# Attention and recurrence steps served in the same turn, value products joined with the next scores, statistics pinned behind the newest matmul, one head pair in another ring of banks

## The chip, the cores and the metric

The kernel runs on one core of one Trainium2 chip. The core has TensorE (PE, matmuls into the eight banks of PSUM), VectorE (DVE), ScalarE (ACT), GpSimd (POOL) and SyncE (SP), each with its own instruction queue, which it works through in order; semaphores tie them together. The metric is the device time of one execution in microseconds: 1956.87 us, the median of 3 runs.

## The reference

One step of a decoder layer for 1024 prompt tokens and 64 sample tokens (8 sequences of 8), model width 1024, all in float32:

```python
x = x + 0.5 * rms_norm(swiglu(rms_norm(x, norm_ffn1_pre), ffn1_w_gu, ffn1_w_down), norm_ffn1_post)
h = rms_norm(x, norm_mix_pre)
z = h @ w_in + b_in                      # q, k, v | hq, hf, hi, hg
a = rms_norm(window_attention(q, k, v, sinks), attn_out_norm)     # 8 heads of 64, 2 key heads, window 128
o = rms_norm(hgrn2_chunked(silu(hq), 1 - f, log f, hi, S0), hg_out_norm) * silu(hg)   # 4 heads of 128 x 128
x = x + rms_norm(concat(a, o) @ w_out, norm_mix_post)
x = x + 0.5 * rms_norm(swiglu(rms_norm(x, norm_ffn2_pre), ffn2_w_gu, ffn2_w_down), norm_ffn2_post)
```

Each feed-forward block has 2816 hidden columns with gate and up weights. The outputs are both token groups, the last 128 keys and values, and the recurrence's states. The sample tokens attend to a cache of 128 positions and start from given states; the prompt attends to its own block of 128 and the one before.

## The kernel before

The tokens form three parts: part 0 with 320 columns (256 prompt tokens and the 64 sample tokens), parts 1 and 2 with 384 prompt tokens each. A product of float32 numbers is made of three matmuls in a reduced format (`mm3`, L242 to L244): both operands are split in a high part (a cast on ScalarE, L219) and a low part (a subtraction on VectorE, L220), and high x high, low x high and high x low are added up in one bank. There are 10242 such matmuls, and they are the stream that everything else is put into. Weights come by DMA into three raw buffers, are split, and lie in a ring of eight tiles (four high and low pairs); a split waits until TensorE has used the pair four places before.

PSUM's eight banks form two rings of four: `mmbank` for the stream, `axbank` for the rest (scores, transposes, values, recurrence, statistics).

The program runs through these stages: the head of the first feed-forward block, twelve hidden tiles for part 0 alone (`up0`), while parts 1 and 2 are normalised (`pre_x`, called from the stream named p1); the rest of its up-projection (`up`); its down-projections (`down`, `pair`); then the middle part, in which projections (`w_in_units`, `w_out_units`), the last down-projections and the head of the second feed-forward block (`f2.head`, again `up0`) run while attention and recurrence are worked off; then the second feed-forward block.

Side work is written as generators, of which each `yield` ends a step. After every 12 matmuls or so (`proj` over four of eight inner tiles) the stream calls `tick`. It advances the named streams by their rates, and by `pace` two queues: "at" (attention blocks, 9 steps each) and "hg" (the recurrence). `pace` adds to each queue's `owed` the rate at which it must go to be done at its due tick (`DUE`), and takes a step of that queue whenever its own `owed` is 1 or more; the two queues are independent.

An attention block (`attn_block`) does its eight heads in two rounds of four. A round computes scores (L1163, two banks), reduces and exponentiates them, transposes the probabilities (L1189, two banks), and multiplies them with the values (L1204, into one bank that both rounds share). Behind the first round's value products stands a `yield`.

`bcast_steps` makes a norm's factor for a part whose tokens lie along the free axis: squares on ScalarE, sums on VectorE, a product with a column of 1/1024 (`st`, L294), then VectorE (L297), a power on GpSimd (L213), a diagonal on VectorE (`dg`, L304), two `yield`s, and a product with ones that spreads the factor over all partitions (`rb`, L308).

The program text does not fix the order on an engine: a scheduler with a model of the machine orders the instructions of each queue as their inputs become ready in that model, and an order that is written as `tc.issue_after(x)` is kept.

Of the kernel before, what the change touches and what calls it, by code (L numbers as in the profile page):

```python
# [18 lines left out]
P = 128  # L19
# [8 lines left out]
NPB = [2, 3, 3]  # L28
# [16 lines left out]
def tile_step(ctx: ExitStack, tc: tile.TileContext, A: dict, O: dict):  # L45
# [63 lines left out]
    def pace():  # L109
        now[0] += 1  # L110
        for k, q in queues.items():
            sofar, rate = 0, 0.0
            for n, _, left in q:
                sofar += left
                rate = max(rate, sofar / max(1, DUE[n] - now[0]))
            owed[k] += rate
            while owed[k] >= 1.0:
                owed[k] -= 1.0
                if q:
                    step(q)  # L120

    def need_mix(n):
        while any(q and q[0][0] <= n for q in queues.values()):
# [116 lines left out]
    def mm3(out, a, b, first, last, resume=False):  # L240

        PE.matmul(out, a[0], b[0], start=first, stop=False, skip_group_check=resume)  # L242
        PE.matmul(out, a[0], b[1], start=False, stop=False, skip_group_check=resume)  # L243
        return PE.matmul(out, a[1], b[0], start=False, stop=last, skip_group_check=resume)  # L244

    def hcol(h, k, w):
        return h[0][k // 4][:, k % 4, :w], h[1][k // 4][:, k % 4, :w]
# [25 lines left out]
    def bcast_steps(part, w, out, q=None, add=None):  # L273

        ss = tmp2("ss")
        for d in range(KC):
            if d == 0:
                S.activation(ss[:, :w], part(d), AF.Square)
                continue
            sq = tmp2("sq")  # L280
            S.activation(sq[:, :w], part(d), AF.Square)  # L281
            (add or V).tensor_tensor(ss[:, :w], ss[:, :w], sq[:, :w], op=ALU.add)
            if d % 3 == 0:
                yield
        yield
        nb = (w + P - 1) // P
        bank = axbank("st")
        sm = small()
        full = w // P
        if w % P:  # L290
            V.memset(sm[:, 0, 0:nb], 1.0)
        for c in range(nb):
            n = min(P, w - c * P)
            PE.matmul(bank[:n, c:c + 1], ss[:, c * P:c * P + n], omean, start=True, stop=True)  # L294
        for r, c in [(P, slice(0, full))] + ([(w % P, slice(full, nb))] if w % P else []):
            if q is None:
                V.tensor_scalar(sm[:r, 0, c], bank[:r, c], EPS, None, op0=ALU.add)  # L297
            else:
                V.scalar_tensor_tensor(sm[:r, 0, c], q[:r, c], EPS, bank[:r, c], op0=ALU.mult, op1=ALU.add)
        root(sm[:, 1, 0:nb], sm[:, 0, 0:nb])  # L300
        dg = tmp2("dg")
        for c in range(nb):
            n = min(P, w - c * P)
            V.tensor_scalar(dg[:, c * P:c * P + n], ident[:, :n], sm[:, 1, c:c + 1], None, op0=ALU.mult)  # L304
        yield
        yield
        rb = axbank("rb")
        PE.matmul(rb[:, :w], ones, dg[:, :w], start=True, stop=True)  # L308
        out.append(rb)
        yield  # L310

# [335 lines left out]
    def make_ffn(wgu, wdn, h, tag):  # L647
# [25 lines left out]
                f.stored = nc.sync.dma_start(acts[:, j], t[:, :w])  # L673
            return rest

        def up0(j, wts, after=None, mid=None):
            w = WIDTH[0]
            g, u = mmbank(), mmbank()
            for bank in (g, u):
                wt = wts.next()  # L680
                parts = (range(4), range(4, 8)) if mid is None or bank is g else (range(4), range(4, 7), range(7, 8))
                for ks in parts:
                    with tc.issue_after(after) if after is not None else nullcontext():
                        r = proj(bank[:, :w], wt, h[0], w, ks)
                    after = after and r.ins
                    if len(ks) == 3:
                        after = mid(after)
                    tick()
                if bank is g and mid is None:
                    rest = gated0(j, g)  # L690
            if mid is not None:
                rest = gated0(j, g)
            rest(u)
# [319 lines left out]
    def mixing(tp, h):  # L1013
# [132 lines left out]
        def attn_block(n, b):  # L1146
# [12 lines left out]
            for pr in range(2):  # L1159
# [37 lines left out]
                for i in range(2):  # L1197
                    for g in range(2):
                        c = (2 * pr + i) * P + 64 * g
                        for kb in range(nk):  # L1200
                            vb = b + kb + (1 if first else 0)
                            for q0 in (0, 64):
                                k1 = (i * nk + kb) * P + q0
                                PE.matmul(ob[q0:q0 + 64, c:c + 64], pT[g][:, k1:k1 + 64],  # L1204
                                          vn[:, vb, g * 64:g * 64 + 64], start=kb == 0, stop=kb == nk - 1)
                if pr == 0:
                    yield
            V.tensor_tensor(sm[:, 2], sinkb, sm[:, 0], op=ALU.subtract)
            S.activation(sm[:, 2], sm[:, 2], AF.Exp)
            V.tensor_tensor(mx[:, 2], mx[:, 1], sm[:, 2], op=ALU.add)  # L1210
# [276 lines left out]
        def ready(kind, n):  # L1487
            if n not in MT:
                MT[n] = new_h(n)
            if kind == "at":  # L1490
                gens = [(attn_block(n, b), 9) for b in range(NPB[n])]
                if n == 0:
                    gens += [(sample_attn(), 11), (kv_out(0), 1)]
                if n == 2:
                    gens.append((kv_out(2), 1))
            else:
                gens = [(intra(n), 8)] + [(hgrn_block(n, b), 3) for b in range(NPB[n])]
                if n == 0:
                    gens.append((sample_hgrn(), 14))
                if n == 2:  # L1500
                    gens.append((state_out(), 1))
# [92 lines left out]
    with tc.tile_pool(name="f1", bufs=1) as tp:  # L1594
# [10 lines left out]
        for i, j in enumerate(first[2:]):  # L1605
            if i == 1:
                with tc.issue_after(f1.stored.ins):
                    xs[2] = load_x(2)
            f1.up0(j, w0)
        f1.begin(units(HEAD1))  # L1610
        need("p1")
        f1.up({6: later(mix_consts), 8: misc, NJ - 1: f1.begin_down})
# [172 lines left out]
```

## Time and profile before

| | |
|---|---|
| runs | 1954.75, 1956.87, 1956.9 us |
| profiled execution | 1956.5 us, span 1954.6 us |
| TensorE busy | 1943.6 us (99%), mean granted clock 0.999 |
| VectorE, ScalarE, GpSimd busy | 1362.4, 929.5, 215.2 us |
| DMA | 358.20 MB, mean 183 GB/s |

The span runs from the first to the last instruction, the execution's time holds some us around it. A row of the timeline has start, duration, engine, line, operation and tiles; in brackets stands idle time of the engine before it and what ended it. In a row of the groups stand busy time and mean duration (ns), then idle time before the group. A matmul's duration overlaps the next one's; the spacing of starts tells the pace.

### The profile page before, as it was taken

The numbers are of one execution on the slowest core, as the hardware profiler recorded it, in microseconds if no ns is written. First come the engines' busy times: TensorE is split into PE (matmuls) and PEld (weight loads), VectorE is DVE, ScalarE is ACT, GpSimd is POOL, SyncE is SP. The second block draws the span as 40 slices with busy tenths as digits, with TensorE's granted clock in tenths as the row PEclk, the third lists the DMA queues.
The fourth block names the chain that finished last, engine by engine and source line by source line (L and its number), as shares of the span: only waits on it lengthen the run. The fifth ranks groups of instructions, "written<-read, shape, count | busy, mean of one in ns | idle before, by whom it ended". The sixth has DMA issues, their size and how long they took to land.

```text
span 1954.6 us, 34186 instructions
## 1 busy us (share of the span) xinstructions
PE 1943.6 (99%) x13469; PEld 1829.0 (94%) x13469; DVE 1362.4 (70%) x2206; ACT 929.5 (48%) x1627; POOL 215.2 (11%) x213
## 2 busy tenths in 40 slices
PE   9999999999999999999999999999999999999998
PEld 9999999999998987788899998999999999999887
DVE  7976667776558666876577576755987877655666
ACT  5533333444455545654345555655544444444453
POOL 0000000000004012121232124011000000000202
PEclk9999999999999999999999999999999999999999
DMA  7443344556767546665434343556555645667874
GB/s 257 147 153 147 134 168 173 183 188 213 245 215 231 183 135 185 214 222 143 132 111 148 97 126 123 165 159 208 171 200 193 217 174 184 210 237 228 309 261 142
DMA packets 160396, 358.20 MB, mean 183 GB/s; under 512 B 16284, under 2 KB 59996, under 8 KB 160220
## 3 DMA queue, kind: packets, MB, share of 16 engines
q1 hardware_dynamic: 159228, 354.19, 54.5%
q8 instruction: 105, 1.72, 0.4%
q10 hardware_dynamic: 1008, 1.84, 0.3%
q14 instruction: 55, 0.45, 0.1%
HBM read 279.33 MB, written 77.63 MB: 183 GB/s over the span
## 4 chain that ended last, share of the span: by engine, by line
PE 97%; DVE 1%; ACT 1%; DMA 0%; issue 0%; SPq 0%; DVEq 0%; POOLq 0%; POOL 0%; ACTq 0%
PE mm L242 29%; PE mm L244 29%; PE mm L243 29%; PE c L242 1%; PE c L244 1%; PE c L243 1%; PE sc L1163 1%; PE pv L1204 1%; PE lv L1237 1%; PE pT L1189 1%; PE av L1338 0%; PE u L1344 0%; PE l L1277 0%; PE av L1341 0%; DMA big<-in_x0T_dram 0%
## 5 line engine op out<-in xcount | busy, mean ns | idle before, releaser
L242 PE MATMUL mm<-h,wsph 128*128 128x320 f32 (+1 forms) x1296 | 416.3, 322 | 2.6 <-ACT sq L281 2.6
L243 PE MATMUL mm<-h,wsph 128*128 128x320 f32 (+1 forms) x1296 | 410.1, 317 | 0.0
L244 PE MATMUL mm<-h,wspl 128*128 128x320 f32 (+1 forms) x1296 | 408.6, 316 | 0.0
L220 DVE TENSOR_TENSOR wspl<-raw,wsph 128x1024 fp32r<-128x1024 f32 x200 | 251.0, 1256 | 151.0 <-ACT wsph L219 146.1
L219 ACT CAST wsph<-raw 128x1024 fp32r<-128x1024 f32 x200 | 209.1, 1047 | 279.2 <-PE mm L243 223.1
L219 ACT CAST w<-raw 128x512 fp32r<-128x512 f32 (+1 forms) x226 | 169.6, 754 | 255.6 <-PE mm L243 127.9
L220 DVE TENSOR_TENSOR w<-raw,w 128x512 fp32r<-128x512 f32 (+1 forms) x226 | 196.5, 873 | 85.2 <-ACT w L219 84.7
L242 PEld LDWEIGHTS mm<-h,wsph 128*128 128x128 f32 x1296 | 244.0, 188 | 10.9 <-issue 6.2
L243 PEld LDWEIGHTS mm<-h,wsph 128*128 128x128 f32 x1296 | 244.1, 188 | 0.8
L244 PEld LDWEIGHTS mm<-h,wspl 128*128 128x128 f32 x1296 | 243.7, 188 | 0.3
L242 PE MATMUL mm<-h,w 128*128 128x384 f32 x704 | 235.6, 335 | 0.0
L243 PE MATMUL mm<-h,w 128*128 128x384 f32 x704 | 235.6, 335 | 0.0
L244 PE MATMUL mm<-h,w 128*128 128x384 f32 x704 | 230.6, 335 | 0.0
L242 PE MATMUL mm<-w,h 128*128 128x512 f32 x462 | 181.2, 395 | 0.0
L243 PE MATMUL mm<-w,h 128*128 128x512 f32 x462 | 180.3, 391 | 0.0
L244 PE MATMUL mm<-w,h 128*128 128x512 f32 x462 | 178.3, 390 | 0.2 <-DVE h L220 0.2
L213 POOL TENSOR_TENSOR sm<-sm,mhalf 128x3 f32<-128x3 f32 (+4 forms) x37 | 37.5, 1013 | 1201.7 <-DVE sm L297 517.7
L242 PEld LDWEIGHTS mm<-h,w 128*128 128x128 f32 x704 | 132.2, 188 | 0.2 <-ACT big L763 0.2
L243 PEld LDWEIGHTS mm<-h,w 128*128 128x128 f32 x704 | 132.1, 188 | 0.0
L244 PEld LDWEIGHTS mm<-h,w 128*128 128x128 f32 x704 | 131.8, 188 | 0.0
L219 ACT CAST w<-t 128x512 fp32r<-128x512 f32 x176 | 106.9, 621 | 49.5 <-PE mm L244 45.8
L220 DVE TENSOR_TENSOR w<-t,w 128x512 fp32r<-128x512 f32 x176 | 118.9, 687 | 11.6 <-ACT w L219 11.6
(339 smaller groups left out, 3686.6 us busy)
## 6 DMA issues: line engine op xcount, KB each, us to landing
raw<-in_ffn_w_gu_dram SPq DMA_DIRECT2D x154, 512.0 KB
raw<-in_ffn_w_down_dram SPq DMA_DIRECT2D x74, 512.0 KB
raw<-in_w_in_dram SPq DMA_DIRECT2D x54, 512.0 KB
ar<-fa SPq DMA_DIRECT2D x70, 384.0 KB
big<-in_ffn_w_down_dram SPq DMA_DIRECT2D x88, 256.0 KB
fb<-big SPq DMA_DIRECT2D x44, 512.0 KB
raw<-fb SPq DMA_DIRECT2D x40, 512.0 KB
fa<-big SPq DMA_DIRECT2D x22, 768.0 KB
```

The costliest lines, as they stand in the source:

```text
L213: G.tensor_tensor(y, x, mhalf[:y.shape[0], :y.shape[1]], op=ALU.pow)
L219: S.copy(hi, src)
L220: return (lo_eng or V).tensor_tensor(lo, src, hi.bitcast(F32), op=ALU.subtract)
L242: PE.matmul(out, a[0], b[0], start=first, stop=False, skip_group_check=resume)
L243: PE.matmul(out, a[0], b[1], start=False, stop=False, skip_group_check=resume)
L244: return PE.matmul(out, a[1], b[0], start=False, stop=last, skip_group_check=resume)
L1163: PE.matmul(banks[g][:, i * 256:i * 256 + wk], zq[64 * g:64 * g + 64, 2 * pr + i, b * P:(b + 1) * P], kx[64 * g:64 * g + 64, k0:k0 + wk], ...
L1189: PE.transpose(bank[:, (i * nk + kb) * P:(i * nk + kb + 1) * P], pt[g][:, i, kb * P:(kb + 1) * P], ident)
L1204: PE.matmul(ob[q0:q0 + 64, c:c + 64], pT[g][:, k1:k1 + 64], vn[:, vb, g * 64:g * 64 + 64], start=kb == 0, stop=kb == nk - 1)
L1237: PE.matmul(b4[ps_, j, a], x[:, a, cs], y[:, a, cs], start=True, stop=True)
```

## The change

Five edits:

1. `pace` no longer serves each queue for itself. When both `owed` together reach 2, or one reaches 1.5, each queue takes one step in the same turn; an empty queue's account is set to 0.
2. In `attn_block` the `yield` behind the first round's value products is gone, so these and the second round's scores belong to one step; the block counts 8 steps.
3. In `bcast_steps` the products `st` and `rb` are pinned behind the matmul of the stream that was written last (`latest`), and a third `yield` stands before `rb`.
4. `up0` takes a function for its banks; the third hidden tile of the first head takes its two banks from `axbank`.
5. `mm3` notes its last matmul in `latest`.

```diff
@@ pace
-            while owed[k] >= 1.0:
+        while sum(owed.values()) >= 2.0 or max(owed.values()) >= 1.5:
+            for k, q in queues.items():
                 owed[k] -= 1.0
                 if q:
                     step(q)
+                else:
+                    owed[k] = 0.0
@@ mm3
-        return PE.matmul(out, a[1], b[0], start=False, stop=last, skip_group_check=resume)
+        r = latest[0] = PE.matmul(out, a[1], b[0], start=False, stop=last, skip_group_check=resume)
+        return r
+
+    latest = [None]
@@ bcast_steps
-            PE.matmul(bank[:n, c:c + 1], ss[:, c * P:c * P + n], omean, start=True, stop=True)
+            with tc.issue_after(latest[0].ins):
+                PE.matmul(bank[:n, c:c + 1], ss[:, c * P:c * P + n], omean, start=True, stop=True)
...
         yield
         yield
+        yield
         rb = axbank("rb")
-        PE.matmul(rb[:, :w], ones, dg[:, :w], start=True, stop=True)
+        with tc.issue_after(latest[0].ins):
+            PE.matmul(rb[:, :w], ones, dg[:, :w], start=True, stop=True)
@@ up0
-        def up0(j, wts, after=None, mid=None):
+        def up0(j, wts, after=None, mid=None, bank_of=mmbank):
             w = WIDTH[0]
-            g, u = mmbank(), mmbank()
+            g, u = bank_of(), bank_of()
@@ attn_block
-                if pr == 0:
-                    yield
@@ ready
-                gens = [(attn_block(n, b), 9) for b in range(NPB[n])]
+                gens = [(attn_block(n, b), 8) for b in range(NPB[n])]
@@ the first head
-            f1.up0(j, w0)
+            f1.up0(j, w0, bank_of=mmbank if i else axbank)
```

Lines behind the edits move by up to 9. How the order on the engines changes is shown at three places; what stands in brackets are the semaphores that an instruction waits for, by the engine that raises them.

The first place is TensorE in the first head, where the third hidden tile begins (`mm_352` and `ax_352` are its gate bank, `rb` the factor of part 0). Before:

```order
L631 MATMUL rb_330<-dg_258,ones 128x320 [waits DVE_49]
L242 MATMUL mm_272<-h_122,wsph_246 128x320
L243 MATMUL mm_272<-h_124,wsph_246 128x320
L244 MATMUL mm_272<-h_122,wspl_247 128x320
L242 MATMUL mm_352<-h_121,wsph_264 128x320 [waits DVE_49,Activation_49]
L243 MATMUL mm_352<-h_123,wsph_264 128x320
L244 MATMUL mm_352<-h_121,wspl_265 128x320
```

Now:

```order
L640 MATMUL rb_330<-dg_258,ones 128x320 [waits DVE_49]
L245 MATMUL mm_272<-h_122,wsph_246 128x320
L246 MATMUL mm_272<-h_124,wsph_246 128x320
L247 MATMUL mm_272<-h_122,wspl_247 128x320
L245 MATMUL ax_352<-h_121,wsph_264 128x320 [waits Activation_49]
L246 MATMUL ax_352<-h_123,wsph_264 128x320
L245 MATMUL ax_353<-h_121,wsph_275 128x320 [waits Activation_49]
L246 MATMUL ax_353<-h_123,wsph_275 128x320
L247 MATMUL ax_352<-h_121,wspl_265 128x320 [waits DVE_49]
```

The first matmul into the bank waits for the cast alone, no longer for VectorE too; the first that waits for VectorE is the one that reads the low part, and two matmuls of the up bank stand ahead of it.

The second place is TensorE and VectorE later in the same head, at the statistics of part 2 (`st_721`, `rb_765` before, `st_733`, `rb_777` now). On TensorE before, 26 matmuls lie between `st` and `rb`; here are the rows around `st`:

```order
L243 MATMUL mm_785<-h_124,wsph_659 128x320
L244 MATMUL mm_785<-h_122,wspl_660 128x320
L242 MATMUL mm_785<-h_122,wsph_659 128x320
L294 MATMUL st_721<-omean,ss_643 128x1 [waits DVE_49,PE_49]
L294 MATMUL st_721<-omean,ss_643 128x1 x2
L243 MATMUL mm_785<-h_124,wsph_659 128x320
```

Now:

```order
L246 MATMUL mm_782<-h_124,wsph_702 128x320
L247 MATMUL mm_782<-h_122,wspl_703 128x320
L301 MATMUL st_733<-omean,ss_664 128x1 [waits DVE_49]
L301 MATMUL st_733<-omean,ss_664 128x1 x2
L317 MATMUL rb_777<-dg_740,ones 128x384 [waits DVE_49]
L245 MATMUL mm_856<-h_121,wsph_749 128x320 [waits DVE_49,Activation_49]
```

On VectorE before:

```order
L297 TENSOR_SCALAR sm_722<-st_721 128x3 [waits PE_49]
L291 MEMSET sm_5681 128x3
L291 MEMSET sm_5863 128x3
L304 TENSOR_SCALAR dg_728<-ident,sm_722 128x128 [waits Pool_49]
L304 TENSOR_SCALAR dg_728<-ident,sm_722 128x128 x2
L668 TENSOR_TENSOR sg_744<-mm_701,rbs 128x320
```

Now (the cast of `wsph_860` waits for the matmul L246 of the rows above, `sg_744` frees the bank that `mm_856` takes):

```order
L304 TENSOR_SCALAR sm_734<-st_733 128x3 [waits PE_49]
L297 MEMSET sm_5681 128x3
L297 MEMSET sm_5897 128x3
L223 TENSOR_TENSOR wspl_861<-raw_858,wsph_860 128x1024 [waits DMAHW2_49,Activation_49]
L311 TENSOR_SCALAR dg_740<-ident,sm_734 128x128 [waits Pool_49]
L311 TENSOR_SCALAR dg_740<-ident,sm_734 128x128 x2
L677 TENSOR_TENSOR sg_744<-mm_698,rbs 128x320 [waits DMAHW0_49]
```

The two products of the statistics stand next to each other, and the split of a weight tile stands between VectorE's first step after `st` and the diagonal.

The third place is the head of the second feed-forward block, near the end of the middle part. On ScalarE before (`sg_13325` is the Silu that reads gate bank `mm_13253`, `h_13353` the cast of half of part 2's normalised tile):

```order
L469 ACTIVATE big_13163<-tr_13246,cols 128x384 [waits PE_49]
L666 ACT_TABLE_LOAD
L666 ACTIVATE sg_13325<-mm_13253 128x320
L1134 ACTIVATE junk,sm_13315<-t_1866_13313 128x512 [waits DVE_49]
L1128 CAST h_10478<-big_11126 128x4x128 [waits DVE_49]
L219 CAST wsph_13409<-raw_13407 128x1024 [waits DMAHW0_49,PE_49,Activation_49]
L666 ACTIVATE sg_13405<-mm_13373 128x320 [waits PE_49]
L483 CAST h_13353<-big_13163 128x1536 [waits DVE_49,Activation_49]
```

Now (`sg_13326` reads gate bank `mm_13262`, which `mm_13439` takes next):

```order
L1201 COPY t_1859_13253<-pT_13248 128x512 [waits PE_49,Activation_49]
L478 ACTIVATE big_13198<-tr_13255,cols 128x384 [waits PE_49]
L222 CAST wsph_13443<-raw_13441 128x1024 [waits DMAHW1_49,PE_49,Activation_49]
L492 CAST h_13353<-big_13198 128x1536 [waits DVE_49,Activation_49]
L675 ACT_TABLE_LOAD
L675 ACTIVATE sg_13326<-mm_13262 128x320
L675 ACTIVATE sg_13405<-mm_13373 128x320
```

And on TensorE now (the cast above waits for VectorE's copy of `tr_13321`):

```order
L247 MATMUL mm_13374<-h_11046,wspl_13267 128x320
L1213 MATMUL pv_13150<-vn_10030,t_1857_13246 64x64 [waits DVE_49]
L1213 MATMUL pv_13150<-vn_10030,t_1857_13246 64x64 x3
L473 MATMUL tr_13321<-ident,big_12313 128x128 [waits PE_49]
L473 MATMUL tr_13321<-ident,big_12313 128x128 x2
L1213 MATMUL pv_13150<-vn_10030,t_1859_13253 64x64 [waits Activation_49]
L1213 MATMUL pv_13150<-vn_10030,t_1859_13253 64x64 x3
L1213 MATMUL pv_13150<-vn_10030,t_1857_13246 64x64 x4
L1213 MATMUL pv_13150<-vn_10030,t_1859_13253 64x64 x4
L245 MATMUL mm_13439<-h_11045,wsph_13330 128x320 [waits Activation_49]
```

The Silu that frees the bank stood ahead of the large cast and stands behind it now, and between the transposes and the matmul that takes the bank stand twelve value products.

Over the whole program the small operations of TensorE form 160 islands between matmuls of the stream before and 141 now.

## The prediction

> **What bounds the kernel now.** I read the head of the page first, then the groups by line, then the waits.
>
> ```profile
> span 1954.6 us, 34186 instructions
> PE 1943.6 (99%) x13469; PEld 1829.0 (94%) x13469; DVE 1362.4 (70%) x2206; ACT 929.5 (48%) x1627; POOL 215.2 (11%) x213
> PE 97%; DVE 1%; ACT 1%; DMA 0%; issue 0%; SPq 0%; DVEq 0%; POOLq 0%; POOL 0%; ACTq 0%
> L242 PE MATMUL mm<-h,wsph 128*128 128x320 f32 (+1 forms) x1296 | 416.3, 322 | 2.6 <-ACT sq L281 2.6
> ```
>
> TensorE is busy 1943.6 of 1954.6 us and is 97% of the chain that ended last. Its main group of matmuls shows one wait in the whole program, 2.6 us. So the time can change in two ways only: TensorE does the same matmuls with less lost at their seams, or it stands still at other places than before. The profiled execution took 1956.5 us, 1.9 more than its span and 0.4 under the median of the runs (1956.87); I make the sum against 1956.5. A measurement of this kernel tells 0.2% (3.9 us) from no change.
>
> The 2.6 us have a place:
>
> ```profile
> 23.85 0.31 PE L243 MATMUL mm<-h,wsph 128*128 128x320 f32 x1
> 24.00 0.31 PE L244 MATMUL mm<-h,wspl 128*128 128x320 f32 x1
> 26.87 0.39 PE L242 MATMUL mm<-h,wsph 128*128 128x320 f32 x1 [2.56 <-ACT sq L281]
> ...
> 24.49 0.49 DVE L632 COPY rbs<-rb 128x320 f32<-128x320 f32 x1
> ...
> 25.16 1.17 DVE L220 TENSOR_TENSOR wspl<-raw,wsph 128x1024 fp32r<-128x1024 f32 x1
> 26.24 0.88 DVE L668 TENSOR_TENSOR sg<-mm,rbs 128x320 f32<-128x320 f32 x2
> ```
>
> The profile names a square of ScalarE as releaser, but matmul 26.87 starts 0.2 us after the first of the two L668 at 26.24 can have ended (0.44 us each). L668 reads the bank that the matmul wants to write; the squares on ScalarE have nothing to do with it. What this stop costs beyond itself is in the stretches around it (span in us, TensorE busy with its count, granted clock, DMA share, GB/s):
>
> ```profile
> 23.78:27.20 3.42, 0.86 (x6) 1.00 0.78 205
> 27.20:30.61 3.41, 3.41 (x15) 0.50 0.71 258
> 30.61:34.02 3.41, 3.41 (x25) 1.00 0.78 239
> ```
>
> In the stretch after the one in which TensorE was busy 0.86 of 3.42 us, its granted clock is 0.50: 15 matmuls where the next stretch holds 25, that is 3.41 / 2 = 1.7 us lost.
>
> **The change part by part.** *A. Head in idle banks.* The pair of banks wanted at 26.87 now comes from the other ring, where two of four banks are unused then. Without the bank, the matmul needs its weights alone:
>
> ```profile
> 17.16 1.98 ACT L219 CAST wsph<-raw 128x1024 fp32r<-128x1024 f32 x2
> 20.23 1.05 ACT L219 CAST wsph<-raw 128x1024 fp32r<-128x1024 f32 x1 [1.09 <-PE st L619]
> ...
> 22.22 2.36 DVE L220 TENSOR_TENSOR wspl<-raw,wsph 128x1024 fp32r<-128x1024 f32 x2
> ```
>
> High parts of both tiles are there at 19.1 and 21.3, low parts at 23.4 and 24.6; the first low part is asked for at about 24.6. So the stop goes: 26.87 - 24.00 - 0.15 (the spacing of these matmuls, 24.00 less 23.85) = 2.7 us, and the slow stretch with it, 1.7: **-4.4**. The other end is -2.7, for a stretch of low clock that not every execution has. What is late next: 48 matmuls later, at about 31.2, TensorE wants the bank that L668 frees at 26.7, so that stays covered.
>
> *B. Statistics pinned behind the newest matmul, one more turn before the broadcast.* Before, between the sum of squares (st) of the third part and its broadcast (rb) lay 26 matmuls of the head. In the new order st and rb stand together, and in VectorE's row the split of a weight tile stands between the first step after st and the diagonal (dg) that rb needs.
>
> ```profile
> 68.06 0.31 PE L242 MATMUL mm<-h,wsph 128*128 128x320 f32 x1
> 68.21 0.72 PE L294 MATMUL st<-omean,ss 128*128 128x1 f32 x6
> 68.79 0.39 PE L243 MATMUL mm<-h,wsph 128*128 128x320 f32 x1
> ...
> 68.97 0.16 DVE L297 TENSOR_SCALAR sm<-st 128x3 f32<-128x3 f32 x1 [1.58 <-PE st L294]
> ...
> 69.21 0.85 POOL L213 TENSOR_TENSOR sm<-sm,mhalf 128x3 f32<-128x3 f32 x1 [29.47 <-DVE sm L297]
> ...
> 70.09 0.68 DVE L304 TENSOR_SCALAR dg<-ident,sm 128x128 f32<-128x128 f32 x3 [0.94 <-POOL sm L213]
> ```
>
> From the start of the last matmul before st (68.06) TensorE goes on after 0.73 us. The diagonal is done after 70.77 - 68.06 = 2.71 at best: a stop of 2.0. With the split between, whose tile is freed by that very matmul: 0.2 until its end, cast 1.05 and split 1.18 (the rows under A), diagonal 0.68, some 0.05 at each hand-over, together 3.25: a stop of 2.5. I take **+2.5** (2.0 to 2.5), as the order puts the split there. Behind rb waits all of TensorE's queue, and VectorE's scaling by rb after it. The second part's broadcast keeps 31 matmuls between, some 4.6 us.
>
> *C. Swapped rows on ScalarE near the end of the middle part.* In the new order the cast of a 128x1536 tile stands before the Silu that reads a head bank; before, it stood six rows behind it. That cast waits for VectorE's copy of three transposes, which TensorE runs just before it wants the bank.
>
> ```profile
> L467 DVE TENSOR_SCALAR big<-tr,cols 128x384 f32<-128x384 f32 x8 | 4.9, 614 | 2.6 <-PE tr L464 2.6
> ...
> L483 ACT CAST h<-big 128x1536 fp32r<-128x1536 f32 x8 | 11.7, 1476 | 2.7 <-DVE big L436 2.1 <-DVE big L495 0.7
> ...
> L666 ACT ACT_TABLE_LOAD x7 | 9.0, 1283 | 0.1
> L666 ACT ACTIVATE sg<-mm 128x320 f32<-128x320 f32 x22 | 9.5, 432 | 0.1
> ```
>
> After the transposes: 0.16 until their result stands, 0.61 + 1.48 + 1.28 + 0.43, with four hand-overs 4.1 us. TensorE has 12 value products left for that time, some 0.9 to 1.0 us (a run of 16 costs 1.28 with both its seams, below). **+3.1** (2.5 to 3.3). That no such stop is in the trace of before agrees with its order, where the Silu was not behind the cast.
>
> *D. Other places.* The pairing moves the small operations of attention and recurrence on VectorE and ScalarE by up to a tick. No transfer is added or removed, SyncE's row has as many issues as before, and ScalarE loads its table 28 times in place of 32. Where these engines have no slack, TensorE stops briefly, as it does now already:
>
> ```profile
> 817.84 0.40 PE L243 MATMUL mm<-w,h 128*128 128x512 f32 x1
> 818.45 0.66 PE L1189 MATMUL pT<-ident,t 128*128 128x128 f32 x4 [0.22 <-DVE h L424]
> 819.32 0.50 PE L244 MATMUL mm<-w,h 128*128 128x512 f32 x1 [0.21 <-DVE h L220]
> ...
> 80.00:100.00 20.00, 20.00 (x138) 20.00 (x137) 20.00 (x19) 13.18 (x14) 0.00 (x0) 1.00 0.47 144
> ```
>
> 1.48 us from the first to the third row, in which four transposes stand that take 0.66 with their run-out: some 0.7 lost. And from 80 to 100 us VectorE is busy 20.00 of 20: a head that comes there 2 us earlier (4.4 less 2.5) may have to give some of it back. Bounds -0.8 (before's own loss goes) and +3; I take **+1.0**, nearest to what one such place costs.
>
> *E. Fewer seams.* Small operations stand as islands in the stream of matmuls. Their price, alone and merged:
>
> ```profile
> 1044.86 0.33 PE L243 MATMUL mm<-h,wsph 128*128 128x384 f32 x1
> 1045.03 0.34 PE L244 MATMUL mm<-h,wspl 128*128 128x384 f32 x1
> 1045.30 1.15 PE L1204 MATMUL pv<-vn,t 128*64 128x64 f32 x32
> ...
> 1046.66 0.34 PE L243 MATMUL mm<-h,wsph 128*128 128x384 f32 x1
> ...
> 1150.54 0.31 PE L244 MATMUL mm<-h,wspl 128*128 128x320 f32 x1
> ...
> 1151.99 0.31 PE L243 MATMUL mm<-h,wsph 128*128 128x320 f32 x1
> ...
> 1157.85 0.31 PE L244 MATMUL mm<-h,wspl 128*128 128x320 f32 x1
> ...
> 1160.38 0.31 PE L243 MATMUL mm<-h,wsph 128*128 128x320 f32 x1
> ```
>
> Value products alone: 1.63 less two spacings of 0.173 = 1.28. Levels alone (1150.54 to 1151.99): 1.45 - 0.29 = 1.16. Both in one island (1157.85 to 1160.38): 2.53 - 0.29 = 2.24. A merge saves 0.20 us. It pays only where two kinds of small products meet that use part of the array (scores, value products, levels). Such meetings are 6 in the order of before and 20 in the new one: 14 x 0.20 = 2.8. Against it, value products are cut by transposes at a few more places; I take **-2.5** (0 to -3.8, the latter if all 19 islands fewer paid).
>
> *F. Low clock after B and C.* The row of 23.78 to 27.20 says that 0.86 us of work in one stretch of 3.4 is too little. A stop of 3.1 leaves no more than that in one stretch in (3.41 - 3.1 + 2 x 0.55) / 3.41 = 41% of the positions that the stretches can have, one of 2.5 at most in 27%. 0.68 x 1.7 = **+1.2** (0 to 3.4).
>
> The Trainium skill, TensorE: Matmul & The Clock Gate (Part 1, the clock gate), has the clock halved after at least one idle window of about 3.4 us. By it neither B nor C would cost any clock and the sum would be 1.2 lower; this trace halved it after a stop of 2.7 us, so the row decides.
>
> Sum: 1956.5 - 4.4 + 2.5 + 3.1 + 1.0 - 2.5 + 1.2 = **1957.4 us**, 0.5 over the median of before.
>
> **The rivals.** *Faster.* B and C do not stand on the chip, or only one: 1956.5 - 4.4 - 2.5 + 1.0 = 1950.6 without both, 1953 to 1954 with one. For it: in the trace of before TensorE nearly never waits, so the order is made with knowledge of such waits. Against it: the chains are made of rows, and TensorE executes its row in order. Chance 0.20.
>
> *Slower, by banks.* A step now issues value products and the next scores at once, and the recurrence's step with them, on a ring of four banks: two for scores, one held for values, one left. The next taker waits for VectorE:
>
> ```profile
> L1171 DVE CUSTOM_DVE_ANT_0 t<-sc,amask 128x256 f32<-128x256 f32 x56 | 20.6, 421 | 5.6 <-PE sc L1163 5.5
> ```
>
> Four of these free a pair of score banks after 1.7 us. If half of that stands open in each of the eight attention blocks, 8 x 0.85 = 6.8 in place of D's 1.0: 1963. It decides from 3.4 us more than the sum on. Against it: the matmuls between two ticks take about as long as those reductions, and the order can put them in between. Chance 0.14.
>
> *The head bank does nothing.* If the idle banks are not idle, or a low part comes late, A's 4.4 stay and the time is 1961.8. The splits end before they are asked for (rows under A). Chance 0.04.
>
> **How the numbers follow.** Forecast 0.62, faster 0.20, slower by banks 0.14, no effect in the head 0.04. Faster by over 0.2% is below 1953.0, slower above 1960.8: faster 0.20, the same 0.62, slower 0.18. The forecast's own range is 1954 to 1960.5 (its bounds not all at one end); with the rivals 1951 to 1962.
>
> **What would show it.** Right: no gap at 24 us and no stretch at 0.50 there; a gap of 2 to 2.5 us before rb near 70 us, released by dg; a gap of about 3 us in the second head, before 1290 us, released by a Silu of ScalarE; 140 islands in place of 160. Wrong: rb and st with matmuls between them; the Silu before the cast; waits of TensorE on score or value banks in most attention blocks; or a loss spread over the whole of the matmuls, which none of these steps can make.

## The result, and the profile after

The changed kernel takes 1965.76 us (median of 6 runs, 1964.02 to 1966.6) where the kernel before takes 1956.59 (6 runs on the same chips): 1.0049 of it, 95% interval 1.0039 to 1.0059. It is 9.2 us slower. The forecast was 1957.4, with 1951 to 1962 around it, and a chance of 0.18 for slower. It was wrong. One execution of e9 below took 5076.84 us beside eleven of 1954.6 to 1959.63 us, and its ratio leaves that one out.

The head of the page of the changed kernel, and all waits of TensorE in it (engine, line, releaser: us in total, times, longest):

```profile
span 1963.4 us, 34164 instructions
PE 1944.5 (99%) x13469; PEld 1832.2 (93%) x13469; DVE 1365.0 (70%) x2206; ACT 922.3 (47%) x1623; POOL 212.8 (11%) x213
```

```profile
PE mm L245 <- ACT sg L675: 3.6, 2, 3.2
PE tr L428 <- DVE h L433: 2.7, 1, 2.7
PE rb L317 <- DVE dg L311: 2.3, 1, 2.3
PE mm L245 <- DVE big L958: 1.2, 1, 1.2
PE mm L544 <- DVE ms L625: 1.1, 1, 1.1
PE mm L246 <- issue: 0.8, 1, 0.8
PE sc L1172 <- issue: 0.3, 1, 0.3
```

TensorE's busy time is up by 0.9 us only, the span by 8.8. The one long wait of before (2.6 us at 24 us) is gone, and three single stops of 2.3 to 3.2 us are there. They lie far apart, and each has one late operand.

**The head** (TensorE's timeline). The third tile starts without a gap, 0.15 us behind its neighbour, in the other ring's banks:

```profile
23.78 0.31 PE L245 MATMUL ax<-h,wsph 128*128 128x320 f32 x1
23.93 0.31 PE L246 MATMUL ax<-h,wsph 128*128 128x320 f32 x1
```

**The first stop** is at 67 us, between st and rb of part 2 (timelines of TensorE, then VectorE; in brackets idle time and what ended it):

```profile
67.18 0.31 PE L247 MATMUL mm<-h,wspl 128*128 128x320 f32 x1
67.33 0.72 PE L301 MATMUL st<-omean,ss 128*128 128x1 f32 x6
70.32 1.30 PE L317 MATMUL rb<-dg,ones 128*128 128x384 f32 x2 [2.27 <-DVE dg L311]
```

```profile
68.09 0.16 DVE L304 TENSOR_SCALAR sm<-st 128x3 f32<-128x3 f32 x1 [1.92 <-PE st L301]
...
68.45 1.23 DVE L223 TENSOR_TENSOR wspl<-raw,wsph 128x1024 fp32r<-128x1024 f32 x1 [0.18 <-ACT wsph L222]
69.60 0.67 DVE L311 TENSOR_SCALAR dg<-ident,sm 128x128 f32<-128x128 f32 x3
```

The split of 1.23 us stands between the first step after st and the diagonal, as the order had it.

**The second stop** is at 818 us, at nine transposes in a row (TensorE, VectorE, GpSimd):

```profile
816.95 0.49 PE L428 MATMUL tr<-ident,big 128*128 128x128 f32 x3
820.17 1.15 PE L428 MATMUL tr<-ident,big 128*128 128x128 f32 x6 [2.72 <-DVE h L433]
```

```profile
814.49 1.19 DVE L1138 TENSOR_TENSOR h<-big,h 128x512 fp32r<-128x512 f32 x1
...
816.20 1.72 DVE L223 TENSOR_TENSOR w<-raw,w 128x1024 fp32r<-128x1024 f32 x1
817.84 1.75 DVE L388 TENSOR_TENSOR big<-big,gb 128x512 f32<-128x512 f32 x1
819.51 0.60 DVE L433 SCALAR_TENSOR_TENSOR h<-tr,cols,h 128x384 fp32r<-128x384 f32 x1
```

```profile
812.92 6.12 POOL L974 TENSOR_TENSOR big<-big,big 128x512 f32<-128x512 f32 x3 [3.19 <-DVE big L958]
```

These are the transposes of the norm before the second feed-forward block. Three of them fill a bank, which ScalarE (L432) and then VectorE (L433) read out, and a split and a gain product, both long, stand ahead of L433.

**The third stop** is at 1289 us in the second head (TensorE, then ScalarE): the cast and the table load stand ahead of the Silu that empties the bank.

```profile
1288.24 0.92 PE L1213 MATMUL pv<-vn,t 128*64 128x64 f32 x24
1292.32 0.42 PE L245 MATMUL mm<-h,wsph 128*128 128x320 f32 x1 [3.17 <-ACT sg L675]
```

```profile
1289.05 1.47 ACT L492 CAST h<-big 128x1536 fp32r<-128x1536 f32 x1 [0.62 <-DVE big L476]
1290.54 1.28 ACT L675 ACT_TABLE_LOAD   x1
1291.83 0.77 ACT L675 ACTIVATE sg<-mm 128x320 f32<-128x320 f32 x2
```

Behind each of the three lies a stretch in which the granted clock is 0.50 (span, TensorE busy with its count, clock, DMA share, GB/s; each pair holds the stretch of the stop and the next one). The clock changes at 70.70, 821.62 and 1292.70 us, 220 and 138 times 3.413 us apart: in this execution the stretches lie on a fixed grid, and a stop falls on it as it happens to come.

```profile
67.29:70.70 3.41, 1.14 (x9) 1.00 0.42 150
70.70:74.11 3.41, 3.41 (x13) 0.50 0.67 200
```

```profile
818.20:821.62 3.42, 1.40 (x9) 1.00 0.60 170
821.62:825.03 3.41, 3.36 (x10) 0.50 0.84 252
```

```profile
1289.29:1292.70 3.41, 0.38 (x2) 1.00 0.44 130
1292.70:1296.11 3.41, 3.41 (x15) 0.50 0.35 125
```

So the span can be accounted for. From the starts of the stream's matmuls I take the time from the last matmul before a group of small products to the first behind it, less one spacing, and compare it with what the same products take where nothing waits; and the time between two neighbouring matmuls, less one spacing.

| | forecast, us | in the trace, us |
|---|---|---|
| A, stop and slow stretch in the head | -4.4 | -4.3 (2.7 + 1.6) |
| B, st and rb | +2.5 | +2.6 |
| C, cast ahead of the Silu | +3.1 | +3.6 |
| D, other stops (those of 811 to 823 us) | +1.0 | +2.1 (4.6 less before's own 2.5) |
| E, seams, with all that is left | -2.5 | +0.1 |
| F, half clock behind the stops | +1.2 | +5.1 (1.49 + 2.07 + 1.56) |
| start of the first matmul | 0 | -0.4 |
| sum | +0.9 | +8.8 |

The 2.07 of F is more than a stretch can lose by half clock alone (3.41 / 2 = 1.7): in it a weight load of TensorE (L247) also waits 0.45 us for a split of VectorE (L223). So F is some 4.7 and not 5.1.

### The profile page after: what moved, and what is told of

Read it like the earlier page. It is cut to its first block, busy times and chain, and to the rows that moved or that the text cites. A ratio compares the mean times of both kernels' runs of the same rounds, so it can differ in the third digit from the quotient of the medians.

```text
span 1963.4 us, 34164 instructions
## 1 busy us (share of the span) xinstructions
PE 1944.5 (99%) x13469; PEld 1832.2 (93%) x13469; DVE 1365.0 (70%) x2206; ACT 922.3 (47%) x1623; POOL 212.8 (11%) x213
## 3 DMA queue, kind: packets, MB, share of 16 engines
q8 instruction: 105, 1.72, 0.4%
q10 hardware_dynamic: 1008, 1.84, 0.3%
## 4 chain that ended last, share of the span: by engine, by line
PE 97%; DVE 1%; ACT 1%; issue 0%; DMA 0%; DVEq 0%; POOLq 0%; POOL 0%; SPq 0%; ACTq 0%
PE mm L245 29%; PE mm L247 29%; PE mm L246 29%; PE c L245 1%; PE c L247 1%; PE c L246 1%; PE sc L1172 1%; PE lv L1244 1%; PE pv L1213 1%; PE pT L1198 1%; PE av L1345 0%; PE mm L544 0%; PE u L1351 0%; PE l L1284 0%; PE av L1348 0%
## 5 line engine op out<-in xcount | busy, mean ns | idle before, releaser
L245 PE MATMUL mm<-h,wsph 128*128 128x320 f32 (+1 forms) x1280 | 410.9, 321 | 3.6 <-ACT sg L675 3.6
L246 PE MATMUL mm<-h,wsph 128*128 128x320 f32 (+1 forms) x1280 | 405.5, 317 | 0.8 <-issue 0.8
L247 PE MATMUL mm<-h,wspl 128*128 128x320 f32 (+1 forms) x1280 | 403.7, 316 | 0.0
L223 DVE TENSOR_TENSOR wspl<-raw,wsph 128x1024 fp32r<-128x1024 f32 x200 | 248.2, 1242 | 146.7 <-ACT wsph L222 145.9
L222 ACT CAST wsph<-raw 128x1024 fp32r<-128x1024 f32 x200 | 209.1, 1047 | 290.4 <-PE mm L246 202.1
L222 ACT CAST w<-raw 128x512 fp32r<-128x512 f32 (+1 forms) x226 | 169.6, 754 | 245.0 <-PE mm L246 110.9
L223 DVE TENSOR_TENSOR w<-raw,w 128x512 fp32r<-128x512 f32 (+1 forms) x226 | 196.6, 874 | 82.9 <-ACT w L222 82.7
L245 PEld LDWEIGHTS mm<-h,wsph 128*128 128x128 f32 x1280 | 241.5, 189 | 9.3 <-ACT sg L675 3.9
L246 PEld LDWEIGHTS mm<-h,wsph 128*128 128x128 f32 x1280 | 241.6, 189 | 3.7 <-issue 3.0
L247 PEld LDWEIGHTS mm<-h,wspl 128*128 128x128 f32 x1280 | 241.1, 189 | 0.1
L246 PE MATMUL mm<-h,w 128*128 128x384 f32 x704 | 235.6, 335 | 0.0
L247 PE MATMUL mm<-h,w 128*128 128x384 f32 x704 | 230.6, 335 | 0.0
L246 PE MATMUL mm<-w,h 128*128 128x512 f32 x462 | 180.5, 391 | 0.0
L247 PE MATMUL mm<-w,h 128*128 128x512 f32 x462 | 178.9, 391 | 0.0
L246 PEld LDWEIGHTS mm<-h,w 128*128 128x128 f32 x704 | 132.1, 188 | 0.0
L247 PEld LDWEIGHTS mm<-h,w 128*128 128x128 f32 x704 | 131.7, 188 | 0.0
L222 ACT CAST w<-t 128x512 fp32r<-128x512 f32 x176 | 106.8, 621 | 47.9 <-PE mm L247 46.0
L223 DVE TENSOR_TENSOR w<-t,w 128x512 fp32r<-128x512 f32 x176 | 118.6, 685 | 11.6 <-ACT w L222 11.6
```

The source lines that it names most:

```text
L222: S.copy(hi, src)
L223: return (lo_eng or V).tensor_tensor(lo, src, hi.bitcast(F32), op=ALU.subtract)
L247: r = latest[0] = PE.matmul(out, a[1], b[0], start=False, stop=last, skip_group_check=resume)
```

## The experiments

Each kernel was timed beside the kernel before on the same chip. The median of before lay between 1955.46 and 1956.38 us.

**One part at a time.** Four kernels, each before with one part of the change.

```diff
 e1: fourth edit alone
-            g, u = mmbank(), mmbank()
+            g, u = bank_of(), bank_of()
...
-            f1.up0(j, w0)
+            f1.up0(j, w0, bank_of=mmbank if i else axbank)
```

> The kernel before with the fourth edit alone: the third hidden tile of the first head takes its two banks from the other ring. Theory as predicted (the stop before rb belongs to the pins and the third turn): the 2.7 us stop at 24 us and the stretch at half clock go and nothing comes, 1956.6 - 4.4 = 1952.2. Rival (the stop before rb is a consequence of the bank): with this edit alone st and rb of part 2 already stand together in TensorE's row, so TensorE stops some 2.5 us near 67 us and runs a stretch at half clock behind it, 2.5 + 1.7 = 4.2: 1956.4, no change, with the rb waiting for dg in the profile.

Measured: 1955.95 us, 0.9999 of before (0.9990 to 1.0008). The rival holds. The stop at 24 us is gone, and TensorE's longest wait is now this one:

```profile
PE rb L308 <- DVE dg L304: 2.3, 1, 2.3
```

At the 110th matmul of the stream this kernel is 4.6 us ahead of the kernel before, at the 380th 5.4; at the 450th, behind rb, 0.7. B is a consequence of the fourth edit; why the order puts st and rb together once the head is earlier is not shown.

```diff
 e2: third and fifth edits alone
+            with tc.issue_after(latest[0].ins):
+                PE.matmul(bank[:n, c:c + 1], ss[:, c * P:c * P + n], omean, start=True, stop=True)
...
+        yield
         rb = axbank("rb")
```

> The kernel before with the third and fifth edits alone: st and rb pinned behind the newest matmul, a third turn before rb. Theory as predicted: st and rb come together, +2.5 and 1.7 for the clock, 1960.8. Rival (the bank): in this kernel's row 26 matmuls still lie between st and rb, as before, so nothing changes: 1956.6 within 1 us, with the stop at 24 us still there.

Measured: 1956.31 us, 1.0001 (0.9992 to 1.0010): nothing, as the rival said. The old stop at 24 us is there, and here the profile names VectorE's L674 (L668 of before) as its releaser and not the squares on ScalarE, which is how the prediction read it:

```profile
PE mm L242 <- DVE sg L674: 2.6, 1, 2.6
```

```diff
 e3: first and second edits alone; e4: the first alone
+        while sum(owed.values()) >= 2.0 or max(owed.values()) >= 1.5:
+            for k, q in queues.items():
...
 e3 and e7 alone
-                if pr == 0:
-                    yield
...
-                gens = [(attn_block(n, b), 9) for b in range(NPB[n])]
+                gens = [(attn_block(n, b), 8) for b in range(NPB[n])]
```

> The kernel before with the first and second edits alone: both queues served in one turn and the turn behind the first value products gone; head and statistics untouched. Theory of single stops: the stop of 3.3 us at the transposes near 817 us (2.1 us more than before's own loss there) and that of 3.6 us before 1290 us are in it, each with 1.7 us of half clock, and some 0.9 spread: 1956.6 + 2.1 + 1.7 + 3.6 + 1.7 + 0.9 - 0.9 = 1965.7 less what the fewer seams bring, so 1963 to 1966, with the stop at 24 us still there. Rival (the stops need the head's 2 us shift or the pins): neither is there, 1955 to 1957.

Measured: 1966.23 us, 1.0050 (1.0036 to 1.0063), above the upper end of the theory's 1963 to 1966. The two stops are there without head bank and pins (2.6 us for L427, 3.2 for the Silu L669).

> The kernel before with the first edit alone: both queues served in one turn, attention blocks of nine steps as before. In ScalarE's row the Silu sg_13326 stands before the cast h_13353 again, so theory of single stops: no stop before 1290 us; scores and levels meet at a few more places (8 in place of 5, 9 islands fewer), worth about 1 us; the place near 815 us stays as uncertain as before's own (0 to 2 us): 1954 to 1958. Rival (serving both queues in one turn is what makes engines late): the loss of the pair of edits is there, 1963 or more.

Measured: 1953.55 us, 0.9985 (0.9976 to 0.9994), just below the theory's range: serving both queues in one turn is a gain of some 3 us. Its eleven runs spread over 5.6 us, and with the mean granted clock of the run:

| mean granted clock | runs, us |
|---|---|
| 0.999 | 1949.91, 1951.34, 1951.75, 1952.41, 1953.55 |
| 0.998 | 1953.10, 1954.19, 1954.77, 1954.84 |
| 0.997 | 1955.33, 1955.52 |

A stretch of 3.41 us at half clock lowers the mean of 1954 us by 0.0009 and costs 1.7 us. The medians of the rows stand 2.7 and 0.9 us apart, which fits that the same order of instructions gets more or fewer such stretches from one execution to the next. The profiled execution (1951.34 us) shows one case: TensorE stops for 2.6 us at 24 us as in the kernel before, but this stop lies across two stretches of the grid and no half clock follows, where before's lay in one stretch with 0.86 us of work:

```profile
21.82:25.24 3.42, 1.93 (x12) 1.00 0.46 133
25.24:28.65 3.41, 2.33 (x16) 1.00 0.93 316
```

**The second edit.** e7 is before with the second edit alone (its diff stands above).

> The kernel before with the second edit alone: the first value products and the second round's scores in one step of eight, queues served apart as before. In ScalarE's row the Silu stands ahead of the cast, as before. Theory (the loss of 10 us needs both edits, since the paired turns of eight steps put the cast ahead of the Silu): no stop before 1290 us, 1954 to 1958, with some loss near 815 us as before. Rival (the longer step alone is what delays VectorE and ScalarE): 1961 or more.

Measured: 1960.52 us, 1.0025 (1.0015 to 1.0035). Neither fits: there is no stop before 1290 us, as the theory has it, but the place near 815 us alone costs 7.4 us from the 4540th to the 4620th matmul, with two stretches at half clock in a row. Of its waits, these belong to that place:

```profile
PE tr L419 <- DVE h L424: 2.9, 1, 2.9
...
PE kT L1331 <- DVE h L424: 1.7, 1, 1.7
PE tr L419 <- DVE big L1316: 1.1, 1, 1.1
```

So the second stop comes with the second edit alone. The third needs both edits: it is in e3, and neither in e4 nor in e7.

```diff
 e12: the change without its second edit
+                if pr == 0:
+                    yield
...
-                gens = [(attn_block(n, b), 8) for b in range(NPB[n])]
+                gens = [(attn_block(n, b), 9) for b in range(NPB[n])]
```

> The changed kernel with its second edit alone undone: the turn behind the first value products is back, a block counts nine steps; paired queues, pins, third turn and head bank stay. Theory (the stops near 817 us and before 1290 us both need the longer step; the head's gain and the stop before rb cancel): 1965.8 less 4.1 for the first and 5.2 for the second with their half clock = 1956.5, less what the paired turns gain by themselves (2.7 against the kernel before): 1953 to 1956, faster than before. Rival (the first edit together with the head's 5 us is enough to make ScalarE's cast or VectorE's evacuations late): 1960 or more, with one of the two stops still there.

Measured: 1954.09 us, 0.9989 (0.9980 to 0.9999), within the theory's range. Both stops are gone, B's is still there:

```profile
PE rb L317 <- DVE dg L311: 2.3, 1, 2.3
...
PE tr L428 <- DVE h L433: 0.6, 1, 0.6
```

Without its second edit the change would have been a small gain; that edit costs 11.7 us in it and 4.5 alone.

**Single stops, mended.**

```diff
 e5: fourth edit, pins, and four turns ahead of rb
         yield
         yield
+        yield
+        yield
         rb = axbank("rb")
```

> The kernel before with the head's third tile in the other ring, the pins, and four turns in place of two between diagonal and rb (one more than the change has). In its TensorE row st of part 2 stands at matmul 404 of the stream and rb some 30 matmuls behind it, where with the bank alone both stood at 384. Theory (the head's gain was lost only because st and rb stood together): no stop at 24 us, none near 67 us, no half clock in the head: 1956.2 - 2.7 to 4.4 - 0.6 = 1951 to 1953. Rival (VectorE, busy 20.0 of 20.0 us from 80 to 100 us, has no slack for a head that comes earlier): the gain is lost at some other place in the head, by waits for splits, 1955 to 1957.

Measured: 1952.51 us, 0.9986 (0.9977 to 0.9995): the theory. The head's gain stays (4.7 us ahead of before from the 450th matmul to the end of the stream), no wait near 67 us is left, and VectorE's full row from 80 to 100 us takes nothing back.

```diff
 e6: the change, the factor's cast pinned behind the newest Silu of its block
-                S.activation(t[:, :w], g[:, :w], AF.Silu)
+                f.sil = S.activation(t[:, :w], g[:, :w], AF.Silu)
...
-        S.copy(hi, src)
+        with tc.issue_after(f.sil.ins) if f.sil is not None else nullcontext():
+            S.copy(hi, src)
```

> The changed kernel with one order mended: in the second head the cast of the 128x1536 factor is pinned behind the newest Silu, so that ScalarE's row has sg_13326 ahead of h_13353. Theory (the 3.2 us stop before 1290 us is TensorE's wait for the bank that this Silu reads, and the cast ahead of it is the cause): that stop falls to under 1 us, its 1.7 us of half clock go, the other two stops stay: 1965.8 - 2.5 - 1.7 = 1961 to 1962. Rival (the cast is late itself, and what follows waits for it, or VectorE is the cause): the stop moves to the next bank or to the reader of the factor: 1964 to 1966.

Measured: 1961.94 us, 1.0033 (1.0021 to 1.0045): the theory. ScalarE's timeline has the Silu ahead, and TensorE's wait falls from 3.17 to 1.07 us (last row):

```profile
1288.55 1.28 ACT L677 ACT_TABLE_LOAD   x1
1289.84 0.44 ACT L677 ACTIVATE sg<-mm 128x320 f32<-128x320 f32 x1
1290.18 1.47 ACT L493 CAST h<-big 128x1536 fp32r<-128x1536 f32 x1
```

```profile
1290.33 0.42 PE L245 MATMUL mm<-h,wsph 128*128 128x320 f32 x1 [1.07 <-ACT sg L677]
```

What still waits there is the table load, which stands directly ahead of the Silu.

**The stop near 817 us.**

```diff
 e9: second edit, one more turn ahead of the gain products
         g = gain_row(gpost, hf)
         yield
+        yield
```

> The second edit alone, with one more turn ahead of a finished half's gain products (L379), so that in VectorE's row these no longer stand between the evacuations of the transposes' banks (L424): what is later by a turn are the gain products and the transposes behind them. Theory (the 7.4 us that the second edit alone loses between 814 and 842 us are TensorE's wait for banks of transposes that VectorE empties late, because gain products and a split stand ahead there): the waits of 1.1, 2.9 and 1.7 us on L424 and L1316 go with their half clock, and the rest of the middle part keeps what it had (-1.4 after that place): 1953.5 to 1956. Rival (the longer step of value products and scores makes VectorE late as such): the stop comes back a turn later, 1959 to 1961.

Measured: 1957.5 us, 1.0009 (1.0001 to 1.0018), between the two: from 1.0025 to 1.0009, some 3 us, come back. TensorE still waits 1.8 us for the evacuation L425 and loses 3.3 us from the 4540th to the 4620th matmul, in place of 7.4. But the added turn did not clear the way. All three gain products (L380) now stand directly ahead of the evacuation for which TensorE waits:

```profile
819.25 2.36 DVE L380 TENSOR_TENSOR big<-big,gb 128x512 f32<-128x512 f32 x3
821.53 0.60 DVE L425 SCALAR_TENSOR_TENSOR h<-tr,cols,h 128x384 fp32r<-128x384 f32 x1
```

ScalarE's half of this evacuation (L424 at 819.44 us) is late too, behind a square that waits 1.51 us for GpSimd's addition. So the 1.8 us that are left don't speak against the theory, and e9 doesn't decide between it and its rival.

```diff
 e10: the change, the additions on VectorE
-                G.tensor_tensor(y2[1][:, i], y2[1][:, i], y2[0][:, i], op=ALU.add)
+                V.tensor_tensor(y2[1][:, i], y2[1][:, i], y2[0][:, i], op=ALU.add)
```

> The changed kernel with the three additions L974 on VectorE instead of GpSimd. In the changed kernel GpSimd's three took 6.12 us, and while they ran the split L223, the gain product L388 and the low part L1138 on VectorE took 1.72, 1.75 and 1.19 us where the same rows take 1.21, 0.68 and 0.69 elsewhere. Theory (VectorE's rows are stretched by GpSimd's work on the same memory): these rows fall back to 1.2, 0.7 and 0.7; the three additions cost VectorE 2.0 us instead of the 2.1 us of stretching, so the stop at the transposes (2.7 us) stays within 1 us: 1964 to 1967. Rival (the rows are long for another reason): L388 and L223 stay at 1.7 and the stop grows by up to 2 us.

Measured: 1965.68 us, 1.0052 (1.0039 to 1.0065), as much as the change. VectorE's rows are short again (0.68, 1.21 and 0.68 where they were 1.19, 1.72 and 1.75), so they were stretched by GpSimd's work; but TensorE still stops for 2.3 us, now for a cast (L222) on ScalarE, which stands behind a square (L384) that waits for the second addition (rows of VectorE, ScalarE and TensorE):

```profile
816.70 1.21 DVE L223 TENSOR_TENSOR w<-raw,w 128x1024 fp32r<-128x1024 f32 x1
...
818.44 0.68 DVE L388 TENSOR_TENSOR big<-big,gb 128x512 f32<-128x512 f32 x1
```

```profile
818.61 0.63 ACT L384 ACTIVATE junk<-big 128x512 bf16<-128x512 f32 x1 [1.33 <-DVE big L974]
...
819.24 0.82 ACT L222 CAST h<-ar 128x768 fp32r<-128x768 f32 x1
```

```profile
820.11 0.50 PE L245 MATMUL mm<-w,h 128*128 128x512 f32 x1 [2.27 <-ACT h L222]
```

No half clock follows this stop (the two stretches that share it hold 1.54 and 2.67 us of work), and up to the 4700th matmul this trace loses 1.2 us less than the change's. The stop before 1290 us then has two stretches at half clock in place of one, which takes the gain back; that the two times are equal is chance in part.

The Trainium skill, SBUF — State Buffer (SBUF: two separate sides), has the port pair that VectorE and GpSimd share as a lock held for a whole instruction. The rows agree that GpSimd's work holds VectorE up (0.68 us becomes 1.75); that a lock is held for a whole instruction no run here shows.

**Putting it together.** e8 is the first and fourth edits without the second and third, with a turn ahead of a factor's cast and one ahead of the gain products:

```diff
 e8
         hi, lo = f.SF[m] = new(), new()
+        yield
         S.copy(hi, src)
...
         g = gain_row(gpost, hf)
         yield
+        yield
```

> The first and fourth edits, without the second and third, and two more turns in other generators: one ahead of a factor's cast, one ahead of the gain products of a finished half. st of part 2 stands at matmul 404 of the stream, rb behind it with matmuls between. Theory (the parts' gains add up once no operand is late): 1956.2 - 2.7 (the first edit alone) - 5.0 (head with its clock) = 1948.5, from 1947 to 1950. Rival (VectorE and ScalarE have no slack and a gain in one place comes back as a wait in another): 1952 to 1956.

Measured: 1948.76 us, 0.9965 (0.9953 to 0.9978): 7.3 us faster than the kernel before, 17.0 faster than the change. It is the fastest of all. Two waits of TensorE are left behind the start of the program, 1.4 us for VectorE's L954 and 0.6 for a split, and no stretch at half clock comes before the end of the stream.

e11 is e8 with the second edit, and e6's pin:

> All that the change does for the side work, mended: first, second and fourth edits, with the two more turns of the fastest kernel so far and the factor's cast pinned behind the Silu. It differs from that fastest kernel (1948.76) by the second edit alone (and the pin). 184 islands by its order in place of 194, and 21 meetings of small products in place of 8. Theory (a merge saves 0.1 to 0.2 us, but a longer step brings waits of its own): 1949 to 1953. Rival (fewer seams pay as forecast, 13 x 0.20 = 2.6): 1946 to 1947.5.

Measured: 1961.89 us, 1.0037 (1.0025 to 1.0049). Both are wrong: the second edit costs 13 us here (with the pin, which no run adds to e8 alone). 21 meetings of small products bring no gain that could be seen, and the waits are back, at other operands than before:

```profile
PE kT L1338 <- DVE h L428: 2.0, 1, 2.0
PE mm L245 <- ACT sg L673: 1.9, 2, 1.6
PE tr L423 <- DVE t L1219: 1.7, 1, 1.7
```

## Why the prediction was wrong

The sum came out some 8 us too low: 3.5 us of it in F, the half clock behind stops, and 3.6 in D, the other stops, with the short waits named under E.

**A (head in idle banks): right**, -4.4 forecast and -4.3 in the trace; the low parts came in time, and e5 keeps the gain to the end.

**B: place, chain and size right (2.5 and 2.6), cause wrong.** The step headed "Statistics pinned behind the newest matmul, one more turn before the broadcast" gave the stop to the third edit. e2 shows that the third edit alone moves nothing in time, and e1 that the fourth alone brings st and rb together. The forecast of the sum doesn't suffer, its reasoning does: A and B are one edit with a net of zero (e1), and the turns, in the right number, are a cure and not the cause (e5: 404th matmul for st, 30 matmuls to rb).

**C: right.** Place, releaser and rows were as forecast, 3.6 for 3.1; e6 takes 3.8 us off by that order alone. Why the cast moved ahead was not asked; it takes the first and second edits together.

**D: mis-sized, and the place that mattered was looked at without its bank.** "I take +1.0, nearest to what one such place costs" took before's row at 817.84 us as the price. The place became the second stop: nine transposes in a row in a ring of four banks, behind evacuations that wait for other rows of VectorE. The bounds of D (to +3) held the 2.1 us, but not the clock behind it, nor the short waits at other places that stand under E: with these D was some 4.6.

**E: the saving didn't reach the total, and its source isn't shown.** "I take -2.5" counted 14 more meetings at 0.20 us each, and the table has +0.1 there. The list of waits tells why. Outside A to D it has 2.7 us in short waits (1.2 for L958, 0.8, 0.3, and 0.4 for L675 beside the third stop), where before had 0.2, and no term of the sum had them. All waits behind the start of the program are 7.7 us longer than before's (10.9 against 3.2) and the half clock costs some 3 more, together nearly 11, but the span grew by 8.8 only. So about 2 us were saved, near the forecast. That the meetings saved them is not shown: worked out in the same way, the change without its second edit (e12) saves some 5 us, and in the traces e12 has 8 meetings of scores, value products and levels where the change has 16 and before 6. In e11, where 13 more meetings than in e8 were to pay 2.6 us, the loss is 13.

**F: mis-sized, +1.2 forecast and some 4.7 found.** The step took the one row at hand, 0.86 us busy of 3.42, as the bound below which the clock falls ("leaves no more than that in one stretch"). The rows after show half clock behind 1.14 and 1.40 us of work too. With a bound of 1.4, a stretch of 3.41 must hold 2.0 us of a stop: for 3.2 us of stop that holds in (3.2 - 2.0 + 1.4) / 3.41 = 76% of the positions, for 2.7 us in 61%, for 2.3 us in 50%, where the prediction had 41% and 27% for its two stops and did not count the one of D at all. That makes 1.9 stretches, 3.2 us; the profiled execution has one behind each of the three stops, so the rest is how these fell on the grid. Nor is 1.4 a sharp bound: half clock also followed 1.60 and 1.84 us of work (e11) and 1.64 (e9), and didn't follow 1.54 (e10) and 1.83 (e6). The Trainium skill, TensorE: Matmul & The Clock Gate (Part 1, the clock gate), asks for an idle window of about 3.4 us; these runs differ, since windows that were busy for a third of their time halved the clock.

**The rivals.** "Slower, by banks" gave 1963 and the right sign, but not the mechanism: the scores (L1172) stand still for 0.3 us in the whole program, and the loss is not spread over eight blocks. Banks decide at one place, and they are those of transposes. "The head bank does nothing" was wrong.

**What stays open.** Why the second edit disturbs so much (4.5 us alone, 11.7 in the change, 13 in e11) is shown only as far as the single waits go. In e10 and e11 one late operand was mended and another stood in its place within a few microseconds, on VectorE or ScalarE. That the longer step bunches these engines' work is an argument that fits; no run isolates it. Nor is it shown what the first edit saves outside waits and clock.

## What to carry to other kernels

Where one engine is 99% busy, look for each single stop and add to it the slow clock that may follow: here three stops of 2 to 3 us cost 8 us and their clock nearly 5 more. A gain of 5 us in one place vanished because two instructions, 26 matmuls apart before, became neighbours: after freeing a bank, look at the order of what comes next. And take a change of several edits apart before explaining it: of these five, one gained 3 us, one lost 4 to 13, and the one that was blamed did nothing.

## What was not expected of the hardware

The clock is halved for a stretch of 3.41 us after one in which TensorE worked 1.14 or 1.40 us, not only after nearly idle ones, and for a second one where the slow stretch itself held a long wait (2.35 us of work in e7, 2.34 in e10). Whether a stop has this price depends on how it falls on the grid of stretches: the same stop of 2.6 us at 24 us has it in the kernel before and not in e4. GpSimd's addition stretched a 128x512 product of VectorE from 0.68 to 1.75 us and a split from 1.21 to 1.72.
